# A one-core decoder block: attention steps in a new order, and the memory's query projection moved ahead as a projection of raw x

## The chip, the cores and the metric

One core of a Trainium2 chip runs the whole kernel. The metric is the device time of one execution in microseconds (us). Its engines are TensorE (PE, matmuls; PEld is its weight load), VectorE (DVE), ScalarE (ACT), GpSimd (POOL) and SyncE (SP), which here only issues DMAs. Each engine works through its own instructions in the order in which the program holds them.

## The reference, cut to what matters

256 tokens, model width 1024, everything in fp32.

```
h = rmsnorm(x, norm_w);  proj = h @ w_in          # q,k,v of mixers A and B, q of the memory, gates, merge logits
o_a = dilated_mixture(three groups of q,k,v)      # mixer A: 8 heads, softmax over 3 dilations together
o_b = moba_attention(q, k, v)                     # mixer B: 8 heads, here one causal block of 256
kv  = rmsnorm(mem, mem_norm_w) @ w_mem_kv
o_m = softmax(q_m k_m^T / 8) v_m                  # memory: 4 heads, 256 memory tokens
p_i = (o_i * silu(gate_i)) @ w_branch_i           # i = a, b, m
x   = x + (sum_i sigmoid(logit_i + b_i) * p_i) @ w_out
out = rmsnorm(x, final_norm_w)
```

## The kernel before

**Weights come in chunks.** The list `PLAN` holds all weight matrices cut into chunks of 128 x 2048 fp32 (1 MB). The main loop takes one chunk per turn `i`. Each chunk is loaded by SyncE (`load`, three buffers `wraw`), then split into two halves of higher and lower bits: ScalarE casts `wh` (L93, three buffers) and VectorE subtracts to get `wl` (L94, two buffers). TensorE then does 48 matmuls of 128x256 for a projection chunk, for each of two output halves n: 16 with `wh` against the high and low part of the activations (L232, L233), then 8 with `wl` (L235). For values (`tok`: Bv, Av, Mv) the three kinds alternate (L252 to L254).

**Raw x first.** A row's norm is one factor per token, so chunks 0 to 5 (q, k, v of mixer B) multiply the raw x (`xh`, `xl`: x times the norm weight) and the factor is put on afterwards by `evac_b`, with `rb["x"]`, the factor spread over all partitions by a matmul (`spread`, L181). The factor comes from `stats` (L167 ff.): ScalarE squares the two halves of `xn` (x loaded once more by token) and sums each row (L171), VectorE and GpSimd make it the power -1/2, VectorE makes a diagonal matrix `dg`. All chunks from 6 on multiply h itself, `hh` and `hl`, in which tokens are reordered into classes (`CLASSES`); VectorE makes them from x and `rb["x"]` (`make_h` L195, `split_h` L199) while TensorE is in chunks 3 to 6.

**Order.** Up to turn 7 a scheduler may move TensorE's instructions; from turn 8 on (`manual_schedule`) TensorE's order is the order of the code. The other engines are ordered by the scheduler throughout. `PLAN` before: Bq (0, 1), Bk (2, 3), Bv (4, 5), gates of b (6, 7), of a (8, 9), of m (10), Mq, the memory's queries (11), Mk (12), Mv (13), then the nine chunks of mixer A for heads 0 to 3 (14 to 22), nine for heads 4 to 7, then merge logits (L), branch outputs (W) and the output (O).

**Attention steps.** Heads go in pairs. A pair has steps: scores (score matmuls into two PSUM banks, tag `s`, two buffers; then softmax on VectorE and ScalarE, result `u`), trans (transposes of `u` on TensorE, 3 or 4 a head, `pt`; ScalarE copies them to `ptsb`) and pv (probabilities times values into one bank `o`, then `gated`). `chain` gives every step a due slot, two slots per chunk, and `pump` runs the due steps, nearly all in the middle of a chunk, between its two halves. With two slots from step to step, scores, trans and pv of a pair stand in three chunks in a row. Where several fall in one slot, the key `-j` puts the later step of the earlier pair first: pv, trans, scores. Mixer A has four steps: scores of the first 128 queries, then their trans and the scores of the others, then trans of these, then pv. Its scores have two kinds of matmul: those of group 0 in split fp32r (`score`, L296, L297), and those of the dilated groups in plain fp32 on 64x64 pieces (L368).

`split_q` and `split_k` make the split operands of `score`: ScalarE casts, VectorE subtracts. For mixer B they run at turns 7 (heads 0 to 3), 10 and 11 (heads 4 to 7) behind the gates' tanh; for the memory's queries directly out of the PSUM of chunk 11 (`Mq11x`).

## Time and profile before

| | |
|---|---|
| time, median of 3 runs (lowest to highest) | 348.95 us (347.75 to 350.6) |
| the profiled execution's own time | 347.43 us |
| its span in the trace | 345.6 us |
| mean granted TensorE clock | 0.994 |
| busy: TensorE, VectorE, ScalarE | 334.7, 233.0, 208.8 us |
| first matmul of a weight chunk, end of the last `y` matmul | 4.41 us, about 337.8 us |

The span runs from the first to the last instruction; 1.83 us of the time lie around it. TensorE is busy for 97% of the span, so idle time and slow spots on TensorE are what can be taken away without fewer matmuls; an idle VectorE or ScalarE by itself costs nothing.

### The profile page before, as it was taken

The numbers are of one execution on the slowest core, as the hardware profiler recorded it, in microseconds if no ns is written. First come the engines' busy times: TensorE is split into PE (matmuls) and PEld (weight loads), VectorE is DVE, ScalarE is ACT, GpSimd is POOL, SyncE is SP. The second block draws the span as 40 slices with busy tenths as digits, with TensorE's granted clock in tenths as the row PEclk, the third lists the DMA queues.
The fourth block names the chain that finished last, engine by engine and source line by source line (L and its number), as shares of the span: only waits on it lengthen the run. The fifth ranks groups of instructions, "written<-read, shape, count | busy, mean of one in ns | idle before, by whom it ended". The sixth has DMA issues, their size and how long they took to land.

```text
span 345.6 us, 7107 instructions
## 1 busy us (share of the span) xinstructions
PE 334.7 (97%) x2924; PEld 321.1 (93%) x2924; DVE 233.0 (67%) x402; ACT 208.8 (60%) x372; POOL 28.8 (8%) x40
## 2 busy tenths in 40 slices
PE   7999999998999999999999999999999999999992
PEld 4989999998999998999999999999999999999882
DVE  3849969999876576576664557676462856658553
ACT  6767858987765657575566357564633564645322
POOL 2502000000211000000101000010000403000022
PEclk9999999999999999999999999999999999999997
DMA  6998694944335434443453355444135467655003
GB/s 205 330 409 326 248 370 158 391 177 166 138 160 177 155 127 161 155 168 132 169 190 112 133 154 214 139 189 162 61 123 184 143 229 247 235 167 199 0 3 122
DMA packets 12945, 63.33 MB, mean 183 GB/s; under 512 B 1392, under 2 KB 2800, under 8 KB 6640
## 3 DMA queue, kind: packets, MB, share of 16 engines
q1 hardware_dynamic: 12912, 62.88, 50.7%
q8 instruction: 23, 0.38, 0.4%
q14 instruction: 10, 0.08, 0.1%
HBM read 61.82 MB, written 1.05 MB: 182 GB/s over the span
## 4 chain that ended last, share of the span: by engine, by line
PE 80%; ACT 6%; DMA 5%; DVE 4%; issue 2%; SPq 1%; POOL 0%; POOLq 0%; DVEq 0%; ACTq 0%
PE pj L232 15%; PE pj L233 14%; PE pj L235 14%; PE pj L252 5%; PE pj L253 4%; PE pj L254 4%; PE pt L320 3%; PE pw L232 3%; PE pw L233 3%; PE pw L235 3%; DMA wraw<-in_wts 3%; DMA xn<-in_x 2%; PE y L491 2%; PE y L492 2%; PE y L493 2%; ACT wh L93 2%
## 5 line engine op out<-in xcount | busy, mean ns | idle before, releaser
L94 DVE TENSOR_TENSOR wl<-wraw,wh 128x1024 fp32r<-128x1024 f32 (+2 forms) x117 | 129.9, 1147 | 54.1 <-issue 36.4
L93 ACT CAST wh<-wraw 128x1024 fp32r<-128x1024 f32 (+2 forms) x117 | 108.1, 968 | 45.9 <-PE pj L233 33.3
L232 PE MATMUL pj<-hh,wh 128*128 128x256 f32 x480 | 114.5, 281 | 0.0
L233 PE MATMUL pj<-hl,wh 128*128 128x256 f32 x480 | 113.3, 278 | 0.5 <-DVE hl L199 0.5
L232 PEld LDWEIGHTS pj<-hh,wh 128*128 128x128 f32 x480 | 90.3, 188 | 1.0 <-issue 0.6
L233 PEld LDWEIGHTS pj<-hl,wh 128*128 128x128 f32 x480 | 90.4, 188 | 0.7 <-DVE hl L199 0.7
L235 PE MATMUL pj<-hh,wl 128*128 128x256 f32 x480 | 64.8, 278 | 0.0
L235 PEld LDWEIGHTS pj<-hh,wl 128*128 128x128 f32 x480 | 59.4, 188 | 0.0
L252 PE MATMUL pj<-wh,hh 128*128 128x256 f32 x96 | 26.9, 281 | 0.0
L253 PE MATMUL pj<-wl,hh 128*128 128x256 f32 x96 | 26.6, 277 | 0.0
L254 PE MATMUL pj<-wh,hl 128*128 128x256 f32 x96 | 26.6, 277 | 0.0
L321 ACT COPY ptsb<-pt 128x384 f32<-128x384 f32 (+1 forms) x28 | 13.2, 497 | 20.7 <-PE pt L320 20.7
L312 ACT ACTIVATE u<-u,st 128x384 f32<-128x384 f32 (+2 forms) x32 | 16.8, 527 | 10.8 <-DVE st L306 10.8
L252 PEld LDWEIGHTS pj<-wh,hh 128*128 128x128 f32 x96 | 18.0, 188 | 0.1
L253 PEld LDWEIGHTS pj<-wl,hh 128*128 128x128 f32 x96 | 18.0, 188 | 0.0
L254 PEld LDWEIGHTS pj<-wh,hl 128*128 128x128 f32 x96 | 18.0, 188 | 0.0
L314 DVE TENSOR_SCALAR u<-u,st 128x256 f32<-128x256 f32 (+2 forms) x40 | 15.5, 396 | 0.9
L354 POOL TENSOR_SCALAR nba<-con 128x512 f32<-128x512 f32 x8 | 5.0, 624 | 125.1 <-DVE st L306 124.8
L492 PE MATMUL y<-wl,mgh 128*128 128x512 f32 (+1 forms) x40 | 13.9, 348 | 0.0
L491 PE MATMUL y<-wh,mgh 128*128 128x512 f32 (+1 forms) x40 | 13.9, 347 | 0.0
L320 PE MATMUL pt<-con,u 128*128 128x128 f32 x88 | 12.7, 278 | 1.2 <-DVE u L314 1.2
L493 PE MATMUL y<-wh,mgl 128*128 128x512 f32 (+1 forms) x40 | 13.9, 346 | 0.0
(195 smaller groups left out, 549.2 us busy)
## 6 DMA issues: line engine op xcount, KB each, us to landing
wraw<-in_wts SPq DMA_DIRECT2D x48, 1024.0 KB, 4.8
wraw<-in_wts SPq DMA_DIRECT2D x15, 256.0 KB, 5.8
xn<-in_x SPq DMA_DIRECT2D x1, 1024.0 KB, 8.6
memT<-in_memT SPq DMA_DIRECT2D x1, 1024.0 KB, 5.5
memn<-in_mem SPq DMA_DIRECT2D x1, 1024.0 KB, 7.7
xres<-in_xr SPq DMA_DIRECT2D x1, 1024.0 KB, 7.6
wraw<-in_wts SPq DMA_DIRECT2D x2, 512.0 KB, 3.3
out<-ysb SPq DMA_DIRECT2D x4, 256.0 KB, 2.1
```

The costliest lines, as they stand in the source:

```text
L93: nc.scalar.copy(whs[i][:, sl], raws[i][:, sl])
L94: lower[i] = nc.vector.tensor_tensor(wls[i][:, sl], raws[i][:, sl], whs[i][:, sl].bitcast(F32), op=ALU.subtract)
L232: nc.tensor.matmul(ps[:, lo:lo + S], wh[:, k, fs], ah[k], start=(k == 0), stop=False)
L233: nc.tensor.matmul(ps[:, lo:lo + S], wh[:, k, fs], al[k], start=False, stop=False)
L235: nc.tensor.matmul(ps[:, lo:lo + S], wl[:, k, fs], ah[k], start=False, stop=(k == kn - 1))
L252: nc.tensor.matmul(ps[:, lo:lo + S], ah[k], wh[:, k, :], start=(k == 0), stop=False)
L253: nc.tensor.matmul(ps[:, lo:lo + S], ah[k], wl[:, k, :], start=False, stop=False)
L254: nc.tensor.matmul(ps[:, lo:lo + S], al[k], wh[:, k, :], start=False, stop=(k == KD - 1))
L320: nc.tensor.transpose(ps[:, P * j:P * (j + 1)], u[:, P * c:P * (c + 1)], ident)
L491: nc.tensor.matmul(y[t, n][:, 0:w], ht, wh[:, k, cs], start=(kc == 0 and k == 0), stop=False)
L492: nc.tensor.matmul(y[t, n][:, 0:w], ht, wl[:, k, cs], start=False, stop=False)
L493: nc.tensor.matmul(y[t, n][:, 0:w], lt, wh[:, k, cs], start=False, stop=(kc == 3 and k == 1))
```

## The change

Four things change together.

1. **Memory queries from raw x.** `Mq` moves from place 11 to place 6 of `PLAN` and multiplies `xh`, `xl` like chunks 0 to 5. Gates of b, a, m move back by one, to 7 to 11. `evac_b` puts the norm on (two VectorE operations, in class order); `split_q` of it follows at turn 13 out of SBUF. Mixer B's `split_q`, `split_k` are now made at turns 8 (heads 0 to 3) and 11 (heads 4 to 7).
2. **Statistics of x on VectorE.** `xn` comes in two DMAs, one a half, and its squares are summed by VectorE (`tensor_tensor_reduce`) and no longer by ScalarE.
3. **Mixer B's scores two chunks ahead of its transposes** (slots 0, 4, 6 from a chunk earlier on), and in a shared slot the key is now (j + 1) modulo the number of steps: pv, scores, trans.
4. **Mixer A**: the second step has the fp32 matmuls of the dilated groups first (`far`), then the transposes, then the split ones (`near`). The last pair's second transposes are cut into two runs of three, half a chunk apart.

```diff
+    out.append(("Mq", 0, "in", 7168))
     for hf in range(2):
         out.append(("G", ("b", hf), "in", 6656 + 256 * hf))
...
-    out.append(("Mq", 0, "in", 7168))
...
-    nc.sync.dma_start(xn, x_d.rearrange("(t p) d -> p t d", p=P))
+    for t in range(2):
+        nc.sync.dma_start(xn[:, t, :], x_d[P * t:P * (t + 1), :])
...
+            if name == "x":
+
+                nc.vector.tensor_tensor_reduce(nat[:, t, :], nat[:, t, :], nat[:, t, :], scale=1.0, scalar=0.0,
+                                               op0=ALU.mult, op1=ALU.add, accum_out=ssq[:, t:t + 1])
+            else:
+                nc.scalar.activation(nat[:, t, :], nat[:, t, :], AF.Square, accum_out=ssq[:, t:t + 1])
...
-        def scores(par):
+        def banks(par):
             if par == 0:
                 for s in range(2):
                     nbs[s] = tp.tile([P, 512], F32, tag="nb", name="nba")
                     nc.gpsimd.tensor_scalar(nbs[s], tab_a, SLOPES_A[2 * pair + s], 1.0, op0=ALU.mult, op1=ALU.mult)
-            banks = [pa.tile([P, 512], F32, tag="s", name="sa") for _ in range(2)]
+            return [pa.tile([P, 512], F32, tag="s", name="sa") for _ in range(2)]
+
+        def near(ps, par):
+
             for s in range(2):
                 if par == 0:
-                    out = banks[s].rearrange("p (a b) -> p a b", a=2)[:, :, 0:P]
+                    out = ps[s].rearrange("p (a b) -> p a b", a=2)[:, :, 0:P]
                 else:
-                    out = banks[s][:, 0:S]
+                    out = ps[s][:, 0:S]
                 score(out, qkv["Aq", hf, 0], qkv["Ak", hf, 0], s, f, slice(P * par, P * (par + 1)), slice(0, S))
+
+        def far(ps, par):
+
             for g in range(1, 3):
                 for s in range(2):
                     rows = slice(HD * s, HD * (s + 1))
                     for r in range(2):
                         ts = slice(P * par + 64 * r, P * par + 64 * (r + 1))
                         lo = P * (par + 1) + 64 * (g - 1)
-                        nc.tensor.matmul(banks[s][64 * r:64 * (r + 1), lo:lo + 64], view("q", g)[rows, f, ts],
+                        nc.tensor.matmul(ps[s][64 * r:64 * (r + 1), lo:lo + 64], view("q", g)[rows, f, ts],
                                          view("k", g)[rows, f, ts], start=True, stop=True)
+
+        def weigh(ps, par):
             for s in range(2):
                 us[s, par] = tp.tile([P, 512], F32, tag="u", name="u", bufs=4)
-                softmax(banks[s], nbs[s][:, P * (1 - par):P * (4 - par)], us[s, par], 0, 384)
-
-        def trans(par):
-            for s in range(2):
+                softmax(ps[s], nbs[s][:, P * (1 - par):P * (4 - par)], us[s, par], 0, 384)
+
+        def first():
+            ps = banks(0)
+            near(ps, 0)
+            far(ps, 0)
+            weigh(ps, 0)
+
+        def second():
+
+            ps = banks(1)
+            far(ps, 1)
+            trans(0)
+            near(ps, 1)
+            weigh(ps, 1)
+
+        def trans(par, heads=(0, 1)):
+            for s in heads:
...
-        return [lambda: scores(0), lambda: (trans(0), scores(1)), lambda: trans(1), pv]
+        if pair == 3:
+            return [first, second, lambda: trans(1, (0,)), lambda: trans(1, (1,)), pv]
+        return [first, second, lambda: trans(1), pv]
...
-    def chain(pairs, first, each):
+    def chain(pairs, first, each, at=(0, 2, 4, 6)):
...
-                steps.append((first + each * n + 2 * j, -j, fn))
+                slot = (0, 2, 4, 5, 6)[j] if len(fns) == 5 else at[j]
+                steps.append((first + each * n + slot, (j + 1) % len(fns), fn))
...
+        if kind == "Mq":
+
+            for n in range(2):
+                cs = slice(S * n, S * (n + 1))
+                nc.vector.tensor_tensor(t[:, cs].rearrange("p (e r i) -> p e r i", e=2, r=2),
+                                        ps[:, cs].rearrange(CLASSES, e=2, r=2),
+                                        rb["x"].rearrange(CLASSES, e=2, r=2), op=ALU.mult)
+            return
...
-        if i in (7, 10):
-            hf = (i - 7) // 3
+        if i in (8, 11):
+            hf = (i - 8) // 3
...
+        if i == 13:
+            with behind_gate(11):
+                qkv["Mq", 0] = split_q(qkv["Mq", 0], -SCALE, "Mq")
-        nat = kind[0] == "B"
+        nat = i < 7
...
-            chain([pair_steps_b(p) for p in range(4)], 2 * i + 14, 2)
+            chain([pair_steps_b(p) for p in range(4)], 2 * i + 12, 2, (0, 4, 6))
```

What this does to the order on the engines, at three places. First, ScalarE at about 15 to 30 us, before: the split of chunk 2 (four pieces), the two squares of `xn`, the split of chunk 3, the copy of the spread factor, the split of chunk 4.

```order
L93 CAST wh_186<-wraw_99 128x512 x4
L171 ACTIVATE xn,ssq_x<-xn 128x1024 x2
L93 CAST wh_251<-wraw_108 128x512 x4
L183 COPY rb_x<-spread_x 128x256
L93 CAST wh_311<-wraw_248 128x1024 x2
```

The same place with the change:

```order
L93 CAST wh_187<-wraw_99 128x512 x4
L93 CAST wh_252<-wraw_109 128x512 x4
L189 COPY rb_x<-spread_x 128x256
L93 CAST wh_312<-wraw_249 128x1024 x2
L93 CAST wh_369<-wraw_310 128x1024 x2
```

The squares are gone from ScalarE, so the casts of chunk 3 follow those of chunk 2 directly. On VectorE they now stand here, behind the `wl` of chunk 2 and ahead of the diagonal matrix (`ISA` is the reduction and the read of its sum):

```order
L94 TENSOR_TENSOR wl_188<-wraw_99,wh_187 128x512 x4
L174 ISA xn,ssq_x<-xn 128x1024
L174 ISA ssq_x 128x1
L174 ISA xn,ssq_x<-xn 128x1024
L174 ISA ssq_x 128x1
L144 TENSOR_SCALAR ssq_x<-ssq_x 128x2
L94 TENSOR_TENSOR wl_253<-wraw_109,wh_252 128x512
L181 TENSOR_SCALAR dg_x<-con,ssq_x 128x128 x2
```

Before, the place of the four `ISA` rows was empty and VectorE waited there for ScalarE.

Second, TensorE in the middle of chunk 13 (Mv), before: the transposes of mixer B's first pair, then the scores of its second pair.

```order
L254 MATMUL pj_1122<-wh_932,ml 128x256
L320 MATMUL pt<-con,u 128x128 x6
L296 MATMUL sb<-Bk0y_646,Bq0x_640 128x256
L297 MATMUL sb<-Bk0z_652,Bq0x_640 128x256
L296 MATMUL sb<-Bk0y_649,Bq0x_643 128x256
L297 MATMUL sb<-Bk0z_655,Bq0x_643 128x256
```

With the change:

```order
L260 MATMUL pj_1162<-wh_926,ml 128x256
L302 MATMUL sb<-Bk1y_936,Bq1x_930 128x256
L303 MATMUL sb<-Bk1z_942,Bq1x_930 128x256
L302 MATMUL sb<-Bk1y_939,Bq1x_933 128x256
L303 MATMUL sb<-Bk1z_945,Bq1x_933 128x256
L302 MATMUL sb<-Bk1y_936,Bq1x_930 128x128
L303 MATMUL sb<-Bk1z_942,Bq1x_930 128x128
L302 MATMUL sb<-Bk1y_939,Bq1x_933 128x128
L303 MATMUL sb<-Bk1z_945,Bq1x_933 128x128
L326 MATMUL pt<-con,u 128x128 x6
```

The scores that stand here are now those of the third pair (`Bk1`, `Bq1`: heads 4 to 7), ahead of the first pair's transposes; those of the first pair have moved to the middle of chunk 11, those of the second to the middle of chunk 12.

VectorE at about the same time, before: the scaling of the first pair's probabilities (`u`, one row pair for each head), and between the heads the `wl` of chunk 14 and Mk.

```order
L313 RECIPROCAL st<-st 128x1 x2
L314 TENSOR_SCALAR u<-u,st 128x256
L314 TENSOR_SCALAR u<-u,st 128x128
L313 RECIPROCAL st<-st 128x1
L94 TENSOR_TENSOR wl_1012<-wraw_930,wh_1011 128x1024 x2
L633 TENSOR_TENSOR Mk<-pj_1015,rb_m 128x512
L313 RECIPROCAL st<-st 128x1
L314 TENSOR_SCALAR u<-u,st 128x256
L314 TENSOR_SCALAR u<-u,st 128x128
```

With the change, from the gate of chunk 11 on:

```order
L696 SCALAR_TENSOR_TENSOR g_1041<-thg,pj_948 128x512
L312 ISA u,st<-sb,nbb 128x256
L312 ISA st 128x1
L312 ISA u,st<-sb,nbb 128x128
L312 ISA st 128x1
L320 TENSOR_SCALAR u<-u,st 128x256
L320 TENSOR_SCALAR u<-u,st 128x128
L94 TENSOR_TENSOR wl_1046<-wraw_924,wh_1045 128x1024 x2
L671 TENSOR_TENSOR Mk<-pj_1049,rb_m 128x512
```

The `wl` of chunk 14 and Mk have moved behind the first pair's last scaling; ahead of it stand a gate and the reductions (`ISA`) of the second pair.

Third, TensorE at the second step of a mixer A pair (`Ak21y`, `Aq20x` are the split operands of group 0, `Ak`, `Aq` the plain ones of the dilated groups), before:

```order
L235 MATMUL pj_2122<-hh,wl_1971 128x256 x8
L320 MATMUL pt<-con,u 128x128 x6
L296 MATMUL sa<-Ak21y_1956,Aq20x_1883 128x256
L297 MATMUL sa<-Ak21z_1962,Aq20x_1883 128x256
L296 MATMUL sa<-Ak21y_1959,Aq20x_1886 128x256
L297 MATMUL sa<-Ak21z_1965,Aq20x_1886 128x256
L368 MATMUL sa<-Ak_1455,Aq_1339 64x64 x4
L368 MATMUL sa<-Ak_1695,Aq_1604 64x64 x4
L232 MATMUL pj_2122<-hh,wh_1970 128x256
```

With the change:

```order
L241 MATMUL pj_2126<-hh,wl_1975 128x256 x8
L380 MATMUL sa<-Ak_1459,Aq_1379 64x64 x4
L380 MATMUL sa<-Ak_1699,Aq_1608 64x64 x4
L326 MATMUL pt<-con,u 128x128 x6
L302 MATMUL sa<-Ak21y_1960,Aq20x_1887 128x256
L303 MATMUL sa<-Ak21z_1966,Aq20x_1887 128x256
L302 MATMUL sa<-Ak21y_1963,Aq20x_1890 128x256
L303 MATMUL sa<-Ak21z_1969,Aq20x_1890 128x256
L238 MATMUL pj_2126<-hh,wh_1974 128x256
```

The plain fp32 matmuls (64x64 pieces and transposes) now stand next to each other, and the split ones next to the chunk's own.

## Rows read from the trace of the kernel before

**Rows 1.** The page: busy time of TensorE in the span, and the granted clock in 40 slices of the span, in tenths.

```profile
PE 334.7 (97%) x2924; PEld 321.1 (93%) x2924; DVE 233.0 (67%) x402; ACT 208.8 (60%) x372; POOL 28.8 (8%) x40
PEclk9999999999999999999999999999999999999997
```

**Rows 2.** The view of waits for TensorE, the whole span: who waited for whom, us in total, times, longest.

```profile
PE pt L320 <- DVE u L314: 1.2, 2, 1.0
...
PE pj L232 <- ACT wh L93: 0.8, 1, 0.8
...
PE pj L233 <- DVE hl L199: 0.5, 1, 0.5
```

**Rows 3.** TensorE in order of time, chunk 3 and the start of chunks 4 and 5: start, duration, operation, tile, [idle before it, and who ended that].

```profile
23.60 0.39 PE L232 MATMUL pj<-xh,wh 128*128 128x256 f32 x1 [0.80 <-ACT wh L93]
...
25.23 0.59 PE L181 MATMUL spread_x<-dg_x,ones 128*128 128x256 f32 x2
...
25.78 0.28 PE L233 MATMUL pj<-xl,wh 128*128 128x256 f32 x1
...
29.75 0.28 PE L252 MATMUL pj<-wh,xh 128*128 128x256 f32 x1
...
35.19 0.28 PE L252 MATMUL pj<-wh,xh 128*128 128x256 f32 x1
```

**Rows 4.** ScalarE in order of time, 20 to 32 us.

```profile
20.85 1.06 ACT L171 ACTIVATE xn<-xn 128x1024 f32<-128x1024 f32 x1 [2.56 <-DMA xn<-in_x]
...
22.95 2.17 ACT L93 CAST wh<-wraw 128x512 fp32r<-128x512 f32 x4
...
26.52 2.00 ACT L93 CAST wh<-wraw 128x1024 fp32r<-128x1024 f32 x2 [0.29 <-DVE wl L94]
29.93 2.01 ACT L93 CAST wh<-wraw 128x1024 fp32r<-128x1024 f32 x2 [1.41 <-DMA wraw<-in_wts]
```

**Rows 5.** VectorE in order of time, 23 to 44 us.

```profile
23.07 0.17 DVE L143 TENSOR_SCALAR ssq_x<-ssq_x 128x2 f32<-128x2 f32 x1 [4.06 <-ACT xn L171]
...
24.19 0.48 DVE L175 TENSOR_SCALAR dg_x<-con,ssq_x 128x128 f32<-128x128 f32 x2
...
27.61 2.69 DVE L94 TENSOR_TENSOR wl<-wraw,wh 128x1024 fp32r<-128x1024 f32 x2 [0.54 <-ACT wh L93]
...
40.95 1.25 DVE L94 TENSOR_TENSOR wl<-wraw,wh 128x1024 fp32r<-128x1024 f32 x1
42.09 1.25 DVE L199 TENSOR_TENSOR hl<-h,hh 128x1024 fp32r<-128x1024 f32 x1
```

**Rows 6.** TensorE in order of time, in chunks 6 and 7, where it first needs the second half of `hl`.

```profile
43.39 0.38 PE L233 MATMUL pj<-hl,wh 128*128 128x256 f32 x1 [0.47 <-DVE hl L199]
```

**Rows 7.** TensorE in order of time, the middle of chunk 13: the six transposes of mixer B's first pair, then the first score matmul of its second pair.

```profile
83.67 0.49 PE L320 MATMUL pt<-con,u 128*128 128x128 f32 x3
85.19 0.55 PE L320 MATMUL pt<-con,u 128*128 128x128 f32 x3 [1.03 <-DVE u L314]
85.50 0.36 PE L296 MATMUL sb<-Bk0y,Bq0x 128*128 128x256 f32 x1
```

**Rows 8.** VectorE in order of time, 61 to 90 us: the memory's statistics, one of two splits of Mq, the `wl` of chunk 14, Mk, the last scaling of mixer B's first pair, two of the four softmax reductions of its second pair.

```profile
61.68 0.17 DVE L143 TENSOR_SCALAR ssq_m<-ssq_m 128x2 f32<-128x2 f32 x1 [0.34 <-ACT memn L171]
...
78.15 0.69 DVE L272 SCALAR_TENSOR_TENSOR Mq11x<-pj,Mq11x 64x512 fp32r<-64x512 f32 x1
...
81.56 2.34 DVE L94 TENSOR_TENSOR wl<-wraw,wh 128x1024 fp32r<-128x1024 f32 x2
83.93 0.69 DVE L633 TENSOR_TENSOR Mk<-pj,rb_m 128x512 f32<-128x512 f32 x1
...
84.61 0.53 DVE L314 TENSOR_SCALAR u<-u,st 128x256 f32<-128x256 f32 x2
...
88.92 0.42 DVE L306 CUSTOM_DVE_ANT_0 u<-sb,nbb 128x256 f32<-128x256 f32 x1
...
89.27 0.28 DVE L306 CUSTOM_DVE_ANT_0 u<-sb,nbb 128x128 f32<-128x128 f32 x1
```

**Rows 9.** TensorE in order of time, the eight transposes of the memory's second pair, in the middle of chunk 20.

```profile
137.07 0.77 PE L320 MATMUL pt<-con,u 128*128 128x128 f32 x5
138.03 0.55 PE L320 MATMUL pt<-con,u 128*128 128x128 f32 x3 [0.20 <-DVE u L314]
138.33 0.36 PE L232 MATMUL pj<-hh,wh 128*128 128x256 f32 x1
```

**Rows 10.** TensorE in order of time, the second step of a mixer A pair, from the end of its six transposes to the chunk's next matmuls.

```profile
163.58 0.36 PE L296 MATMUL sa<-Ak21y,Aq20x 128*128 128x256 f32 x1
163.79 0.28 PE L297 MATMUL sa<-Ak21z,Aq20x 128*128 128x256 f32 x1
...
164.03 0.28 PE L297 MATMUL sa<-Ak21z,Aq20x 128*128 128x256 f32 x1
164.24 0.46 PE L368 MATMUL sa<-Ak,Aq 64*64 64x64 f32 x16
164.63 0.38 PE L232 MATMUL pj<-hh,wh 128*128 128x256 f32 x1
164.85 0.29 PE L233 MATMUL pj<-hl,wh 128*128 128x256 f32 x1
```

**Rows 11.** Groups of VectorE instructions by line and shape, the whole span: busy us, mean ns of one | idle before.

```profile
L306 DVE CUSTOM_DVE_ANT_0 u<-sa,nba 128x384 f32<-128x384 f32 x16 | 8.3, 555 | 7.9 <-PE sa L368 7.9
```

More of the change, by code (lines that the diff above doesn't have):

```diff
@@ L170, in stats @@
         for t in range(2):
-            nc.scalar.activation(nat[:, t, :], nat[:, t, :], AF.Square, accum_out=ssq[:, t:t + 1])
+            if name == "x":
[3 more added lines that the diff above has]
+                nc.scalar.activation(nat[:, t, :], nat[:, t, :], AF.Square, accum_out=ssq[:, t:t + 1])
         r = rstd_of(ssq, name)
@@ L571 @@
                 split(i + 2, j, 4 if i < 2 else 2)
-        if i in (7, 10):
-            hf = (i - 7) // 3
+        if i in (8, 11):
+            hf = (i - 8) // 3
             with behind_gate(i - 1):
                 qkv["Bqx", hf] = split_q(qkv["Bq", hf], 1.0, f"Bq{hf}")
-                if i == 7:
-                    qkv["Bkx", hf] = split_k(qkv["Bk", hf], f"Bk{hf}")
-        if i == 11:
-            with behind_gate(9):
-                qkv["Bkx", 1] = split_k(qkv["Bk", 1], "Bk1")
+                qkv["Bkx", hf] = split_k(qkv["Bk", hf], f"Bk{hf}")
         if i in (9, 10):
@@ L614 @@
                         split(i + 2, 1, 2)
-        if kind[0] == "B":
+        if i < 7:
             late.append((i, kind, key) + ((pss[2 * i], pss[2 * i + 1]) if i < 2 else (ps, None)))
@@ L620 @@
                     late.remove(z)
-                if i > 3:
+                if i in (4, 5):
                     split_h(4 * i - 16, 4 * i - 12)
```

## The prediction, made before the change was run

> **What bounds the kernel now.** I read the page first: TensorE is busy for 97% of the span at full granted clock until the last slice [rows 1], so the time is TensorE's own work plus the few places where it stands. The waits of TensorE alone [rows 2] name three engines' work it waited for: transposes for VectorE's scaled probabilities, a projection for ScalarE's weight cast, another for VectorE's `hl`. These three sum to 2.5 us; beside them it waits only in its first 6 us, which the change leaves alone. So no order of steps can bring more than this and what TensorE loses around the waits. I then read each place in order of time on TensorE and on the engine it waits for [rows 3 to 9], and last the places where TensorE never waits and still is slower than its pitch [rows 10]. The pitch: chunk 4 has 48 matmuls and runs from 29.75 to 35.19 [rows 3], 5.44 us, or 0.113 us a matmul. The number of matmuls does not change, so the gain is the sum of the stalls that go, less those that come.
>
> **A. Start of chunk 3.** TensorE was ready at 22.80 and began at 23.60 behind ScalarE's cast; chunk 4 began at 29.75 [rows 3], 6.95 us later than 22.80. Needed are 48 x 0.113 = 5.44 and the spread matmul, 25.78 - 25.23 less one pitch = 0.44: 5.88 together. So 1.07 us are lost: 0.80 of waiting, and 0.27 in which casts of 2.17 / 4 = 0.54 each pace matmuls that want a piece every 0.46. ScalarE was late because it squared `xn` from 20.85 to 22.95, after waiting 2.56 us for xn's DMA [rows 4]. Without the squares it can cast as soon as chunk 3 lands. That landing has no row; all four pieces were there when the casts ran from 22.95 on without a pause, and a cast begun by 22.26 is in time.
> The new risk is the spread matmul, which now stands behind 8 of chunk 3's matmuls, so TensorE comes to it at 22.80 + 0.91 = 23.71. It needs the diagonal matrix, which was ready at 24.19 + 0.48 = 24.67, 1.6 us after the sums at 23.07 [rows 5]. No row shows a VectorE reduction of 1024 elements. Nearest are the softmax reductions, 0.28 us at 128 columns, 0.42 at 256 [rows 8], 0.555 at 384 [rows 11]: 0.14 for each further 128 gives 1.26. VectorE is free from 23.07 - 4.06 = 19.01. If the first half of xn has landed by 19.6 (my estimate: one half of the DMA earlier than the whole, which landed at 20.85) and the second lands with the whole, the sums end at 20.85 + 1.26 + 0.1 = 22.2 and the diagonal at 23.8: a wait of 0.1. If both halves land only at 20.85, the sums end at 23.5, the diagonal at 25.1, a wait of 1.4. I take the first.
> Then chunk 4 sets the limit. ScalarE's first cast of it began at 26.52 after a wait put down to VectorE's `wl`, but that `wl` is chunk 3's, which this cast doesn't need; so it was chunk 4's own DMA, which doesn't move. VectorE's first half of `wl` follows at 27.61 + 1.25 = 28.86 [rows 5], TensorE wants it with its second matmul: chunk 4 begins at 28.75 at the earliest. **Gain 1.0** of 1.07; bounds 1.07 and -0.35.
>
> **B. `hl` in chunk 6.** TensorE waited 0.47 us and its next matmul was 0.10 slower [rows 6]: 0.57. The memory's queries now fill this place with raw x and need no `hl`. VectorE's order from 27.61 to 43.34 is unchanged and starts from the same DMA, so `hl` ends at 42.09 + 1.25 = 43.34 as before [rows 5], while chunk 7, which wants it, begins at 28.75 + 3 x 5.44 = 45.1: covered by 1.7 us. Chunk 6 itself wants the second half of its `wl`, ready at 40.95 + 1.25 = 42.2, at its 23rd matmul, 39.63 + 2.5 = 42.1: a wait of 0.1 at most. The two new VectorE operations that put the norm on replace, later, the reading of PSUM in two splits of 0.69 [rows 8]; VectorE has time for them. **Gain 0.6**, bounds 0 and 0.6. TensorE is then 1.6 us ahead.
>
> **C. First transposes of mixer B.** Three transposes took from 83.67 to 85.19, the next three 0.31 [rows 7]: 1.2 us lost. Whether it comes back is VectorE's affair, which hardly pauses from 61.68 to the end of that scaling at 84.61 + 0.53 = 85.14 [rows 8]. In the new order this stretch loses two splits of Mq (2 x 0.69), the `wl` of chunk 14 (2.34) and Mk (0.69), 4.4 us; it gains the second pair's reductions (2 x 0.70) and one gate (as Mk, 0.69), 2.1 us. It ends at 85.14 - 2.3 = 82.8 if it begins at 61.68 again, which hangs on ScalarE's squares of `mem` and its queue of casts. TensorE comes to the middle of chunk 13 at 83.67 - 1.6 + 0.9 (one more group of 8 score matmuls stands ahead) = 83.0; first the third pair's scores, which need the second pair's reductions out of the way of the PSUM banks (82.8 - 0.53 = 82.3, cover 0.7), then at 83.9 the transposes (cover 1.1). Behind the scores no one waits but TensorE itself and all its projections. **Gain 1.2**, less 0.2 for a cover this thin; bounds 1.2 and the loss of the slow rival below.
>
> **D. Transposes of the memory's second pair.** Eight took 138.33 - 137.07 = 1.26; at 0.10 each, as the last three [rows 9], they take 0.8. The scores of that pair now go ahead of the first pair's transposes, so its softmax starts some 0.8 us earlier, more than the wait. **Gain 0.4**, bounds 0 and 0.46.
>
> **E. Fewer changes between plain fp32 and split matmuls.** In a second step of mixer A, the matmul behind the transposes takes 163.79 - 163.58 = 0.21 instead of 0.12, the first plain one 164.24 - 164.03 = 0.21, and back 164.85 - 164.63 = 0.22 [rows 10]: three changes of 0.09 to 0.10. With `far` and the transposes side by side two are left. Counting stretches of plain work on TensorE in both orders, mixer A has 18 before and 13 now (with one more for the cut transposes), mixer B 5 and 6. Four stretches fewer at 0.09 to 0.19 are 0.4 to 0.75 us. **Gain 0.4**; bounds 0 (if the cost hangs on the shape alone) and 0.75.
> [...]
>
> **Sum.** 1.0 + 0.6 + 1.2 - 0.2 + 0.4 + 0.4 = 3.4 us. Against the profiled execution: 347.43 - 3.4 = 344.0. That execution lies 1.5 us under the median of 348.95, and the change has nothing to alter that scatter, so the median comes to **345.6**. Nothing after the memory's pairs but E changes, and the 1.83 us outside the span stay.
>
> **Rivals.**
> *Squares slow on VectorE.* If a reduction with both inputs in SBUF runs at half speed, 2.5 us each, the second ends at 24.7, the diagonal comes at 26.3 and TensorE waits 2.6 us: 345.6 + 2.6 = 348.2. For it: no row has such an operation. Against: subtractions with both inputs in SBUF take 1.25 at 1024 [rows 5], as the extrapolation. [...] Chance 0.13.
> *The stall moves.* TensorE, 1.6 us earlier, meets a VectorE and DMAs that are no earlier from 27 to 45 us: any of the covers of 0.1 in A and B that fails hands the gain back. Then A and B bring 0.2: 345.6 + 1.4 = 347.0. For it: VectorE runs there without a pause. Chance 0.13.
> *VectorE late in chunk 13, slower than before.* If ScalarE's casts keep the second pair's reductions at their old time, 89.27 + 0.28 = 89.55 [rows 8], the third pair's scores find no bank and TensorE stands from 83.0 on for 6.5 us: 345.6 + 6.5 = 352.1. It is slower than before from a wait of 3.4 us on. Against: 2.3 us of work have been taken out from ahead of them. Chance 0.04.
>
> **How the numbers follow.** The forecast has 0.70, its own range 344.4 to 346.8 (E at its bounds, C without its 0.2, half a us of scatter). For 8 in 10 the range goes from 343.9 (all gains at their upper bounds, scatter) to 348.1, which takes in the two rivals that lose the start. One per cent, about what a measurement of this kernel tells from none, is 3.5 us, under 345.46: the forecast lies on that edge, a little above. So faster by over 1% gets 0.43 of it, slower by over 1% (above 352.4) 0.03, within 0.54.
>
> **What would show it.** On TensorE no wait before chunk 3, in chunk 6 and in the middles of chunks 13 and 20; chunk 4 beginning near 28.75; the spread matmul without a wait of over 0.2; the sums of x ended by 22.3; two slow changes a second step. Wrong would be a reduction of 1024 columns near 2.5 us, a wait of TensorE at scores of mixer B, or a new one for `wl` between 28 and 50 us.

## The result, and the profile after

The changed kernel takes 345.75 us (median of 6 runs, 344.76 to 347.16), the kernel before beside it 348.75: a ratio of 0.992 (0.990 to 0.995). A second comparison gave 345.52 against 348.20, 0.992 (0.988 to 0.995). So it is 2.7 to 3.0 us faster, 0.8%, and the forecast of 345.6 came true to 0.15 us. How it came true is another matter: the forecast's own sum ran from the profiled execution, 347.43, to 344.0, and the changed kernel's profiled execution took 346.01. One of the five terms brought nothing, the saving of another was taken back, and what decides most was not among them. The intervals leave out two executions, of 1178 and 676 us, that stand far above all others of their kernels.

The page of the changed kernel, the rows that answer to [rows 1]:

```profile
PE 335.4 (97%) x2924; PEld 322.2 (94%) x2924; DVE 235.9 (69%) x408; ACT 206.3 (60%) x368; POOL 28.8 (8%) x40
...
PEclk9999999999999999999999999999999999999997
```

And the view of waits for TensorE, to set beside [rows 2] (us in total, times, longest):

```profile
PE pwarm L138 <- DVE zero L108: 1.0, 1, 1.0
PE pj L251 <- ACT wh L93: 0.6, 1, 0.6
PE spread_x L187 <- DVE dg_x L181: 0.2, 1, 0.2
```

All three waits of [rows 2] are gone: `u`, `hl` and ScalarE's cast ahead of chunk 3. New is 0.2 us at the spread matmul (0.1 was forecast); the 0.6 us is for weights of the first chunk that landed late, and ends at 10.6 us. Yet TensorE's busy time, which holds no waits, *rose* from 334.7 to 335.4 us, at a mean granted clock of 0.994 in both spans. That row points at what decides the case.

To see where the time went I cut the trace of each kernel at the same four places on TensorE: the start of chunk 4, the end of the memory's last pv, the end of mixer A's last pv (each taken as the start of the matmul behind it), and the first output matmul.

| us | first projection to chunk 4 | to the memory's end | to mixer A's end | to the output |
|---|---|---|---|---|
| before | 25.34 | 115.43 | 109.01 | 62.68 |
| changed | 25.35 | 114.14 | 108.20 | 62.68 |
| changed, second profile | 24.99 | 114.14 | 108.20 | 62.68 |

The first stretch swings from run to run; the others come out the same to 0.01 us in the two profiles of the changed kernel, and so they tell tenths apart that no median can. The gain is 1.29 between chunk 4 and the memory, 0.81 in mixer A, and nothing at the start or the end: 2.10, and TensorE's last matmul starts 1.98 earlier on the clock of the two profiles (338.91 and 336.93; its end in the kernel before, which the table ahead of the prediction puts at about 337.8, lies at 339.2). The end of VectorE's last scaling moved by 2.27, since VectorE's last wait for ScalarE shrank from 0.81 to 0.52, but the span by 1.4 only: what follows that scaling, the last output transfer, took 0.85 us longer. This is no scatter. The view of DMA queues from the issue of the last two output transfers to the end (queue: packets, MB, share of 16 engines), before and then changed:

```profile
q1 hardware_dynamic: 288, 0.52, 39.7%
```

```profile
q1 hardware_dynamic: 288, 0.52, 31.7%
q14 instruction: 1, 0.01, 1.2%
```

In the changed kernel a load of 8 KB of instructions falls into the output transfer. It does so in seven of the 13 profiles of this document, and there the last transfer lands 2.8 to 3.0 us after its issue; in the other six that load starts 0.9 us or more ahead of these issues, and the transfer lands after 2.05 to 2.06. The seven are both profiles of the changed kernel and those of its variants that keep the squares on VectorE and the queries on raw x; the six are the kernel before, its variants, and the three kernels below that have the squares or the queries put back. No run moves the load by itself, so that it is the cause is argued and not shown; but a span set against one of those three is off by some 0.9 us in their favour. The medians say 2.7 to 3.0; what is over 2.3 of that has no place in the traces.

**The start of chunk 3.** The changed kernel's ScalarE, then VectorE, then TensorE in order of time, to set beside [rows 3 to 5]:

```profile
22.22 2.53 ACT L93 CAST wh<-wraw 128x512 fp32r<-128x512 f32 x4 [2.95 <-DMA wraw<-in_wts]
...
26.68 2.00 ACT L93 CAST wh<-wraw 128x1024 fp32r<-128x1024 f32 x2 [0.80 <-DMA wraw<-in_wts]
```

```profile
19.93 1.23 DVE L174 CUSTOM_DVE_ANT_0 xn<-xn 128x1024 f32<-128x1024 f32 x1
...
21.28 1.23 DVE L174 CUSTOM_DVE_ANT_0 xn<-xn 128x1024 f32<-128x1024 f32 x1
...
24.18 0.48 DVE L181 TENSOR_SCALAR dg_x<-con,ssq_x 128x128 f32<-128x128 f32 x2 [0.61 <-POOL ssq_x L145]
```

```profile
23.51 0.28 PE L238 MATMUL pj<-xh,wh 128*128 128x256 f32 x1
...
24.81 0.67 PE L187 MATMUL spread_x<-dg_x,ones 128*128 128x256 f32 x2 [0.22 <-DVE dg_x L181]
...
29.87 0.28 PE L258 MATMUL pj<-wh,xh 128*128 128x256 f32 x1
```

The reductions of 1024 columns take 1.23 us (the extrapolation gave 1.26) and end at 22.51. ScalarE casts chunk 3 as soon as it lands, at 22.22. But TensorE comes to chunk 3 only at 23.51, 0.7 later than the 22.80 of before, held up by weights in its first 20 us. ScalarE's casts of chunk 2, before (the first piece of this row is still chunk 1's) and then changed, end at 15.04 + 3.25 = 18.29 and 16.67 + 2.61 = 19.28:

```profile
15.04 3.25 ACT L93 CAST wh<-wraw 128x512 fp32r<-128x512 f32 x5 [1.38 <-DMA wraw<-in_wts]
```

```profile
16.67 2.61 ACT L93 CAST wh<-wraw 128x512 fp32r<-128x512 f32 x4 [0.63 <-DMA wraw<-in_wts]
```

And the diagonal matrix is ready at 24.18 + 0.48 = 24.66, no earlier than before (24.67 [rows 5]): VectorE waited 0.61 us for GpSimd's power, which took 1.27 us instead of 0.72 (GpSimd's spans are rough). From start to start the spread matmul held TensorE up 0.46 us more than before. So chunk 4 begins at 29.87 against 29.75 [rows 3].

**Mixer B and the memory.** TensorE at the places of [rows 7] and [rows 9]:

```profile
85.95 0.84 PE L326 MATMUL pt<-con,u 128*128 128x128 f32 x6
...
136.52 1.09 PE L326 MATMUL pt<-con,u 128*128 128x128 f32 x8
137.36 0.37 PE L238 MATMUL pj<-hh,wh 128*128 128x256 f32 x1
```

The six transposes go in one run, and the eight take 137.36 - 136.52 = 0.84 instead of 1.26.

**What was not in the sum.** In both kernels the matmuls of a projection follow each other at one of two intervals, and keep to it for a whole block. The row that holds the last eight matmuls of a block is 1.07 us long at the one and 1.11 at the other; from start to start it is 113.3 ns (10.88 us for 96) and 117.8 (11.31 for 96). TensorE in chunks 6 to 8, before and then changed:

```profile
47.01 1.07 PE L235 MATMUL pj<-hh,wl 128*128 128x256 f32 x8
48.71 1.07 PE L235 MATMUL pj<-hh,wl 128*128 128x256 f32 x8
51.43 1.07 PE L235 MATMUL pj<-hh,wl 128*128 128x256 f32 x8
```

```profile
45.70 1.11 PE L241 MATMUL pj<-xh,wl 128*128 128x256 f32 x8
...
51.12 1.11 PE L241 MATMUL pj<-hh,wl 128*128 128x256 f32 x8
53.95 1.11 PE L241 MATMUL pj<-hh,wl 128*128 128x256 f32 x8
```

The changed kernel runs chunks 6 to 10 and half of 11, 264 matmuls, at the longer interval: 264 x 4.5 ns = 1.2 us, of which the kernel before pays less than 0.1, for the 18 matmuls of chunk 6 ahead of its wait for `hl`. It eats more than that wait had cost (0.57).

### The profile page after: what moved, and what is told of

Its sections match the earlier page's. It is cut to its first block, busy times and chain, and to the rows that moved or that the text cites. A ratio compares the mean times of both kernels' runs of the same rounds, so it can differ in the third digit from the quotient of the medians.

```text
span 344.2 us, 7110 instructions
## 1 busy us (share of the span) xinstructions
PE 335.4 (97%) x2924; PEld 322.2 (94%) x2924; DVE 235.9 (69%) x408; ACT 206.3 (60%) x368; POOL 28.8 (8%) x40
## 4 chain that ended last, share of the span: by engine, by line
PE 90%; DMA 5%; DVE 1%; SPq 1%; POOL 1%; issue 0%; POOLq 0%; DVEq 0%
PE pj L238 17%; PE pj L241 17%; PE pj L239 17%; PE pj L258 5%; PE pj L260 5%; PE pj L259 5%; PE pt L326 3%; DMA wraw<-in_wts 3%; PE pw L238 3%; PE pw L239 3%; PE pw L241 3%; DMA xn<-in_x 2%; PE y L522 2%; PE y L523 2%; PE y L524 2%; PE oa L415 1%
## 5 line engine op out<-in xcount | busy, mean ns | idle before, releaser
L238 PE MATMUL pj<-hh,wh 128*128 128x256 f32 x464 | 110.8, 280 | 0.0
L239 PE MATMUL pj<-hl,wh 128*128 128x256 f32 x464 | 109.6, 278 | 0.0
L238 PEld LDWEIGHTS pj<-hh,wh 128*128 128x128 f32 x464 | 87.4, 188 | 0.7 <-issue 0.6
L239 PEld LDWEIGHTS pj<-hl,wh 128*128 128x128 f32 x464 | 87.4, 188 | 0.0
L241 PE MATMUL pj<-hh,wl 128*128 128x256 f32 x464 | 62.8, 278 | 0.0
L241 PEld LDWEIGHTS pj<-hh,wl 128*128 128x128 f32 x464 | 57.6, 188 | 0.0
L312 DVE CUSTOM_DVE_ANT_0 u<-sa,nba 128x384 f32<-128x384 f32 x16 | 8.3, 555 | 7.1 <-PE sa L303 3.8
```

The source lines that it names most:

```text
L238: nc.tensor.matmul(ps[:, lo:lo + S], wh[:, k, fs], ah[k], start=(k == 0), stop=False)
L239: nc.tensor.matmul(ps[:, lo:lo + S], wh[:, k, fs], al[k], start=False, stop=False)
L241: nc.tensor.matmul(ps[:, lo:lo + S], wl[:, k, fs], ah[k], start=False, stop=(k == kn - 1))
```

## The experiments

### One part undone at a time

Four kernels, each the changed one with one part put back.

```diff
 # squares of x back on ScalarE
-            if name == "x":
-                nc.vector.tensor_tensor_reduce(nat[:, t, :], nat[:, t, :], nat[:, t, :], ...)
-            else:
-                nc.scalar.activation(nat[:, t, :], nat[:, t, :], AF.Square, accum_out=ssq[:, t:t + 1])
+            nc.scalar.activation(nat[:, t, :], nat[:, t, :], AF.Square, accum_out=ssq[:, t:t + 1])
```

> The changed kernel with the squares of x back on ScalarE (x still comes in two halves). By my step A (the squares held up ScalarE's casts of chunk 3) TensorE waits some 0.8 us for a cast ahead of chunk 3 again, chunk 4 begins about 1.0 us later than 29.87, and the time rises from 345.75 to about 346.7. By the rival (the landing of the weights of chunks 3 and 4 paces TensorE there, whoever squares) the wait before chunk 3 may return, but chunk 4 begins within 0.2 us of 29.87 and the time stays within 0.3 us.

Measured: 344.83 us, 0.991 (0.988 to 0.993); no slower than the changed kernel. The wait is back, and chunk 4 does begin 1.5 us later than in the changed kernel. TensorE:

```profile
24.92 0.39 PE L233 MATMUL pj<-xh,wh 128*128 128x256 f32 x1 [0.85 <-ACT wh L93]
...
31.35 0.28 PE L253 MATMUL pj<-wh,xh 128*128 128x256 f32 x1
```

Half a us of that came before chunk 3, and the next stretch is shorter: 113.40 against 114.14, because here chunks 4 and 5 ran at 117.8 ns and chunks 6 to 10 at 113.3. TensorE's way from the first projection to the last output matmul is 1.2 us longer (333.64 against 332.42). So neither theory was right: the wait costs, but the profile's time does not show it, for the interval gave back 0.74, and the last output transfer, without the load of instructions, 0.9.

```diff
 # the memory's queries back behind the gates (and Bq, Bk splits at chunks 7, 10, 11)
-    out.append(("Mq", 0, "in", 7168))
     for hf in range(2):
         out.append(("G", ("b", hf), "in", 6656 + 256 * hf))
...
     out.append(("G", ("m", 0), "in", 7424))
+    out.append(("Mq", 0, "in", 7168))
...
```

> The changed kernel with the memory's queries back in their old place behind the gates, made from the normalized hh and hl, and the splits of mixer B's queries and keys back at their old chunks. By my step B the first matmul on hl stands in chunk 6 again, waits 0.4 to 0.5 us for VectorE and is 0.1 slower: the time rises by 0.6 to about 346.3, and nothing else waits, since VectorE's two splits (2 x 0.69) fit into the 1.7 us that it has in hand at mixer B's third scores. By the rival (the cover there is used up) a wait on VectorE of 0.3 to 1.5 us comes on top near 85 us: 346.6 to 347.8. By a third reading (what is gained at hl is lost again in the next chunks) the wait returns and the time does not change.

Measured: 345.34 us, 0.992 (0.989 to 0.994). The wait for `hl` is there, 0.45 us, and no wait for VectorE came with it; by the medians the time did not change. The trace says more: the stretch from chunk 4 to the memory's end takes 115.21 us instead of 114.14. Ahead of the wait chunk 6 ran at 113.3 ns (15 matmuls in 1.70 us), behind it at the long interval, as did chunks 7 to 10:

```profile
43.79 0.39 PE L239 MATMUL pj<-hl,wh 128*128 128x256 f32 x1 [0.45 <-DVE hl L205]
44.72 1.10 PE L241 MATMUL pj<-hh,wl 128*128 128x256 f32 x8
```

So undoing B cost 1.07 us here. The profile's span hides it (344.3 us against 344.2): this kernel's last output transfer, too, is without the load of instructions.

```diff
 # mixer B's old slots and order
-            chain([pair_steps_b(p) for p in range(4)], 2 * i + 12, 2, (0, 4, 6))
+            chain([pair_steps_b(p) for p in range(4)], 2 * i + 14, 2, old=True)
...
```

> The changed kernel with mixer B's steps in their old slots and order: scores one chunk ahead of their transposes. By my step C the first transposes of the mixer wait about 1.0 us for VectorE's scaling again: 345.75 + 1.2 = 346.9 or so. By the rival (it is the memory's queries, taken out of VectorE's stretch from 61 to 85 us, that made u early: 85.14 less two splits of 0.69 is 83.8, when TensorE comes at 83.7 to 84.0) they wait 0.3 us at most, and the time stays within 0.4 us.

Measured: 347.79 us, 0.9995 (0.997 to 1.002): 2.0 us lost, more than expected. TensorE waits twice for `u`:

```profile
84.82 1.01 PE L326 MATMUL pt<-con,u 128*128 128x128 f32 x6 [1.11 <-DVE u L320]
...
93.91 0.30 PE L326 MATMUL pt<-con,u 128*128 128x128 f32 x1 [0.71 <-DVE u L320]
```

The second wait is one that the kernel before doesn't have. VectorE shows why: between the second pair's reductions and its last scaling now stand the splits of the memory's queries, which the change has put at chunk 13, and the `wl` of a chunk:

```profile
89.19 1.49 DVE L278 SCALAR_TENSOR_TENSOR Mqx<-Mq,Mqx 64x512 fp32r<-64x512 f32 x2
...
90.85 2.34 DVE L94 TENSOR_TENSOR wl<-wraw,wh 128x1024 fp32r<-128x1024 f32 x2
...
93.24 0.99 DVE L320 TENSOR_SCALAR u<-u,st 128x256 f32<-128x256 f32 x4
```

So the place of the queries' splits suits the new slots and not the old ones; the rival, that the slots don't matter, is out.

```diff
 # mixer A's second step as before, no cut of the fourth pair's transposes, the old order in a shared slot
+            trans(0)
             ps = banks(1)
+            near(ps, 1)
             far(ps, 1)
-            trans(0)
-            near(ps, 1)
...
-        if pair == 3:
-            return [first, second, lambda: trans(1, (0,)), lambda: trans(1, (1,)), pv]
...
-            chain([pair_steps_a(2 * key[0] + p) for p in range(2)], 2 * i + 2, 4)
+            chain([pair_steps_a(2 * key[0] + p) for p in range(2)], 2 * i + 2, 4, old=True)
```

> The changed kernel with mixer A's steps as before: transposes, near, far in the second step, the old order of steps that fall on one slot, and the last transposes of the fourth pair in one step. By my step E five stretches of plain fp32 work come back at 0.09 to 0.19 each: 0.4 to 0.7 us, 346.2 to 346.5. [...] From the second steps' own times in the two traces (1.62 before, 1.58 after) I would rather expect 0.03 to 0.1 a step, 0.1 to 0.3 in all.

Measured: 346.21 us, 0.9945 (0.992 to 0.997), 0.46 us above the changed kernel's 345.75, with an interval that overlaps that one's. The stretch to mixer A's end tells it apart: 109.21 us against 108.20, 1.0 us, of which 0.4 is that 374 instead of 285 matmuls have the long interval, and 0.6 the changes. E's lower bound of 0, for a cost that hangs on the shape alone, is out; so is my 0.1 to 0.3. In the changed kernel's second step, the matmul behind the transposes (same 128x128 shape, another type) still holds up its successor by 163.36 - 163.16 = 0.20, 0.09 more than the pitch:

```profile
162.53 0.87 PE L326 MATMUL pt<-con,u 128*128 128x128 f32 x6
163.16 0.37 PE L302 MATMUL sa<-Ak21y,Aq20x 128*128 128x256 f32 x1
163.36 0.28 PE L303 MATMUL sa<-Ak21z,Aq20x 128*128 128x256 f32 x1
```

### Two parts undone at once, one part done alone

The changed kernel with the first two edits above together:

> The changed kernel with two parts undone at once: the squares of x on ScalarE and the memory's queries in their old place. By my steps A and B this costs 1.0 + 0.6 = 1.6 us, a ratio of about 0.9965 to the kernel before, and the two waits (0.8 for ScalarE's cast ahead of chunk 3, 0.5 for hl in chunk 6) are back. By the reading that each of the two undone alone suggests (ratios of 0.9909 and 0.9917 against 0.9923 for the whole) they cost nothing: 0.992, though the waits are back. A third reading: one hides the other, so that only the later wait costs: 0.6, about 0.9935.

Measured: 345.85 us, 0.993 (0.990 to 0.996), beside 345.52 for the changed kernel in the same comparison. The wait for `hl` has grown, since this time the start was quick (24.63 us to chunk 4), and behind it the matmuls are at the short interval:

```profile
43.41 0.38 PE L234 MATMUL pj<-hl,wh 128*128 128x256 f32 x1 [1.09 <-DVE hl L200]
...
47.05 1.07 PE L236 MATMUL pj<-hh,wl 128*128 128x256 f32 x8
48.75 1.07 PE L236 MATMUL pj<-hh,wl 128*128 128x256 f32 x8
```

The stretch from chunk 4 takes 114.41 us with a wait of 1.09, and 114.14 without any. The wait and the slow matmuls beside it cost 1.4 us, of which 1.1 came back: 257 matmuls at the long interval instead of 502. For the wait turned the interval here from long to short; with the queries alone put back it turned it from short to long, and a shorter wait cost 1.07.

> The changed kernel as it is, on the chip of the next three, so that all four have one measure. 345.75 give or take 0.5, 0.992 of the kernel before. In its profile the matmuls of chunks 4 to 10 should again follow at one of two intervals, 113.3 or 117.8 ns, and which of them rules from about 16 to 72 us need not be the one of the first profile (117.8 from chunk 6 on): if it is chance, another profile can differ there by up to 1.5 us.

The changed kernel again gave 345.52 and the same interval in the same chunks. But it hangs on the start. Two kernels of this document, the one with mixer A's old steps and the one below with the split matmuls last, have the same order on TensorE until 154 us; both began chunk 4 at the long interval, and their stretches to the memory's end took 114.55 and 113.40 us instead of 114.14.

```diff
 # the kernel before, with mixer B's new slots alone
-            chain([pair_steps_b(p) for p in range(4)], 2 * i + 14, 2)
+            chain([pair_steps_b(p) for p in range(4)], 2 * i + 12, 2, (0, 4, 6), True)
```

> The kernel before with one part of the change alone: mixer B's scores two chunks ahead of its transposes, in the order pv, scores, transposes. By my step C, as sized, 1.2 us less than before: 0.9965. By what its undoing cost (2.0 us, two waits on u of 1.11 and 0.71), 2 us less: 0.994. By the rival of VectorE late in chunk 13 (here the memory's queries are still in VectorE's way) the third pair's scores wait for a bank: a wait of TensorE at scores of over 0.5 us, and 0.998 or more.

Measured: 346.66 us, 0.996 (0.994 to 0.998), 1.5 us less than before. The stretch from chunk 4 is 114.09 instead of 115.43: 1.34, of which 0.3 is a shorter wait for `hl` (0.2 instead of 0.47, after a late start). No scores waited; the transposes still waited 0.2. This is step C by itself, at 1.0, or 1.2 with the interval taken out (284 matmuls at the long one instead of 258).

### The interval

Tabulating in the traces which interval ruled ahead of each step and which behind, I had a guess that steps which end in plain fp32 make the next block slow. So I put the split matmuls last (`far`, then `near` in the first step, with the third step's transposes ahead of it, and the cut dropped):

```diff
-            near(ps, 0)
             far(ps, 0)
+            near(ps, 0)
...
-        if pair == 3:
-            return [first, second, lambda: trans(1, (0,)), lambda: trans(1, (1,)), pv]
...
-            chain([pair_steps_a(2 * key[0] + p) for p in range(2)], 2 * i + 2, 4)
+            chain([pair_steps_a(2 * key[0] + p) for p in range(2)], 2 * i + 2, 4, rank=(2, 2, 1, 0))
```

> The changed kernel with mixer A's first step turned round (far ahead of near), the third step's transposes ahead of it, and the fourth pair's last transposes in one run again: wherever near stands, it is the last of its step. In the traces so far a projection block behind a step that ends in plain fp32 has its matmuls at 117.5 to 122 ns, one behind near at 113.3 to 113.5. If the last matmul of a step sets that, the blocks behind the four first steps (2 of 48, 2 of 24 and 24 more each) speed up by 4 to 8 ns a matmul and two stretches go: about 1.0 to 1.4 us less than the changed kernel, 344.5. If the cost is only that of the changes between plain and split (0.1 to 0.2 each), one or two of which go: 0.1 to 0.3 less. [...]

Measured: 347.71 us, 0.999 (0.997 to 1.001): 2.2 us *slower* than the changed kernel. No expectation held. Mixer A's stretch was as in the changed kernel (108.29), but the last one took 65.11 us instead of 62.68. Every projection from 251 us on had the long interval. The table of transitions, read again, is of another kind: a run of six plain transposes by itself *turns* the interval, whichever it was (18 times of 18 over the 13 profiles of this document); a run of three leaves it (16 of 16); between two blocks with no step between them it stays (in all 473 places from chunk 4 on), except where a chunk with the activations as weights is followed by one with the weights as weights, where it mostly turns (91 of 106). That gave two predictions with opposite signs.

```diff
 # the changed kernel, the fourth pair's last six transposes in one run
-        if pair == 3:
-            return [first, second, lambda: trans(1, (0,)), lambda: trans(1, (1,)), pv]
```

> The changed kernel with one edit: the fourth pair's last six transposes in one step again, not in two runs of three. By the count of stretches in my step E a plain stretch less should save 0.1 to 0.2 us: 345.4. By the reading of the eight traces so far (a run of six transposes turns the interval of the matmuls behind it from 113.3 to 117.8 ns or back, a run of three leaves it, and nothing turns it again from some 252 us to the end of the projections at 315) all 528 matmuls there now run at 117.8 ns: 2.4 us more, about 347.9, and the stretch from mixer A's last pv to the output chunks takes 65.1 instead of 62.7 us.

Measured: 348.74 us, 1.000 (0.998 to 1.003): the whole gain gone. The last stretch takes 65.11 us. TensorE around the cut and at the start of two later blocks, 96 matmuls apart, in the changed kernel and then with one run of six:

```profile
243.60 1.07 PE L241 MATMUL pj<-hh,wl 128*128 128x256 f32 x8
244.51 0.49 PE L326 MATMUL pt<-con,u 128*128 128x128 f32 x3
...
246.67 1.07 PE L241 MATMUL pj<-hh,wl 128*128 128x256 f32 x8
247.58 0.49 PE L326 MATMUL pt<-con,u 128*128 128x128 f32 x3
...
255.05 0.28 PE L238 MATMUL pj<-hh,wh 128*128 128x256 f32 x1
...
265.93 0.28 PE L238 MATMUL pw<-ogm,wh 128*128 128x256 f32 x1
```

```profile
245.07 1.07 PE L241 MATMUL pj<-hh,wl 128*128 128x256 f32 x8
245.98 0.82 PE L326 MATMUL pt<-con,u 128*128 128x128 f32 x6
...
248.52 1.11 PE L241 MATMUL pj<-hh,wl 128*128 128x256 f32 x8
...
256.79 0.28 PE L238 MATMUL pj<-hh,wh 128*128 128x256 f32 x1
...
268.09 0.28 PE L238 MATMUL pw<-ogm,wh 128*128 128x256 f32 x1
```

The same 96 matmuls take 265.93 - 255.05 = 10.88 and 268.09 - 256.79 = 11.30 us. It is not the granted clock: the view by stretches of that kernel (stretch, its length, TensorE's busy time and instructions, granted clock, DMA share, GB/s) has it at 1.00, as the changed kernel's has:

```profile
256.50:267.50 11.00, 11.00 (x95) 1.00 0.43 146
```

```profile
256.50:267.50 11.00, 11.00 (x99) 1.00 0.41 144
```

The kernel before, with the cut and nothing else:

```diff
+        if pair == 3:
+            return [lambda: scores(0), lambda: (trans(0), scores(1)), lambda: trans(1, (0,)), lambda: trans(1, (1,)), pv]
...
```

> The kernel before with one edit: the fourth pair's last six transposes cut into two runs of three, as the change has them. There the projection ahead of them runs at 117.8 ns and the one behind at 113.3. By the same reading the cut takes away the turn, the matmuls to the end stay at 117.8 ns, and the kernel is 2.4 us slower than before, a ratio of 1.007. By the count of stretches one is added: 0.1 to 0.2 us, 1.0005. If the cut makes TensorE fast by itself: no change, since it is fast there already.

Measured: 351.15 us, 1.007 (1.004 to 1.010), as the turning says. The block ahead of these transposes is slow in the kernel before; one run of six turns it to fast for all that follows, and the cut takes that away (65.12 us for the last stretch). So by the last stretch the same edit is worth 2.4 us in one order and costs 2.4 in the other. Last, the place where the interval turned in chunk 6:

```diff
+            if n == "v" and hf:
+                out.append(("Mq", 0, "in", 7168))
             out.append(("B" + n, hf, "in", b0 + 512 * i + (256 * hf if i else 0)))
-    out.append(("Mq", 0, "in", 7168))
...
```

> The changed kernel with the memory's queries between the two chunks of mixer B's values instead of behind them, so that the step from a chunk with the weights moving to one with the weights standing, which turned the interval in 65 of 80 places, comes twice instead of once ahead of the gates. If chunk 4 begins at 113.3 ns, then chunks 5 and 6 are slow and 7 to 10 fast, instead of 6 to 10 slow: 0.7 to 0.8 us less, 344.8, with the stretch from chunk 4 to the memory's pairs shorter by that. If chunk 4 begins at 117.8 ns, it is chunks 5 and 6 that are fast and 7 to 10 slow: 0.6 us more than the changed kernel would take from that start. If the interval has nothing to do with such steps: the same time, 345.6.

Measured: 345.20 us, 0.990 (0.987 to 0.993), not to be told from the changed kernel by medians. The stretch from chunk 4 is 113.44 instead of 114.14, 0.70 less, as expected, and TensorE shows the two halves of chunk 5 slow and those of chunk 7 fast:

```profile
37.64 1.10 PE L242 MATMUL pj<-xh,wl 128*128 128x256 f32 x8
40.47 1.11 PE L242 MATMUL pj<-xh,wl 128*128 128x256 f32 x8
...
48.94 1.07 PE L242 MATMUL pj<-hh,wl 128*128 128x256 f32 x8
51.66 1.07 PE L242 MATMUL pj<-hh,wl 128*128 128x256 f32 x8
```

With the interval known, the lengths of the stretches can be freed of it. In each trace I counted the matmuls of projections whose successor starts some 117.8 ns later, and took 4.5 ns off for each:

| us | chunk 4 to the memory's end | long ones | freed | to mixer A's end | long ones | freed |
|---|---|---|---|---|---|---|
| before | 115.43 | 258 | 114.27 | 109.01 | 329 | 107.53 |
| changed | 114.14 | 502 | 111.88 | 108.20 | 285 | 106.92 |
| squares back | 113.40 | 336 | 111.88 | 108.20 | 284 | 106.92 |
| memory's queries back | 115.21 | 580 | 112.60 | 108.20 | 285 | 106.92 |
| both back | 114.41 | 257 | 113.26 | 108.20 | 283 | 106.92 |
| mixer B's old slots | 116.32 | 481 | 114.16 | 108.20 | 285 | 106.92 |
| before, mixer B's new slots alone | 114.09 | 284 | 112.81 | 109.00 | 328 | 107.52 |
| mixer A's old steps | 114.55 | 598 | 111.86 | 109.21 | 374 | 107.53 |
| split matmuls last | 113.40 | 337 | 111.88 | 108.29 | 282 | 107.01 |

Freed of the interval, kernels that share a part agree on it to 0.02 us. The change takes 114.27 - 111.88 = 2.39 us of waits and slow matmuls out of the first stretch and 0.61 out of the second; the interval gives 1.1 of the first back and adds 0.2 to the second.

## Why the prediction was right, and where it was not

The number held because errors cancelled. Of the 3.4 us of the sum, A brought nothing; B, C and D together brought 2.39 instead of 2.0, and E 0.6 instead of 0.4. Against these 3.0 stand 0.9 lost to the interval and 0.85 at the last output transfer, neither of which was in the sum, and the profiled span shrank by 1.4. That the medians moved by 2.7 to 3.0 all the same, and met the forecast, is luck as far as the traces go.

- **A, start of chunk 3** (gain 1.0): the mechanism held, the gain did not show. ScalarE's cast no longer waits for squares, and the reduction's 1.23 us confirm the extrapolation, so the rival of slow squares is out: no run shows the 2.5 us that it took for a reduction at half speed. The step that failed is the one that took TensorE's arrival at chunk 3 (22.80; it came at 23.51) and the diagonal (23.8; it was ready at 24.66) for settled. Over 13 profiles the way from the first projection to chunk 4 took 25.7 us on average with the squares on ScalarE (24.6 to 27.3, five profiles) and 25.5 with them on VectorE (24.7 to 27.2, eight): it swings by more than the term, so that no gain of A can be told from these. The sums came at 22.5, not 22.2, for the second half of `xn` landed at 21.26 and not by 20.85; the wait at the spread matmul was 0.2, and 0.46 from start to start.
- **B, `hl`** (0.6): the wait went, no cover failed; chunk 7 came late enough. Freed of the interval, the wait with its slow matmuls costs 0.72 where it is 0.45 long and 1.38 where it is 1.09, so the term was right. But "the stall goes" is not "the time goes": the wait had turned the interval in chunk 6, in the kernel before to the short one, and without it TensorE stayed at 117.8 ns. Undoing B cost 0.27 us (with the squares put back too) where chunk 4 had begun at the short interval, and 1.07 where it had begun at the long one.
- **C, mixer B** (1.2 less 0.2): 1.0 alone (1.2 freed of the interval), and 2.18 by undoing it (116.32 against 114.14), because the queries' splits, moved to chunk 13, make a second wait in the old order. The term was right for the step by itself; that the parts lean on each other was left out. The covers of 0.7 and 1.1 were wider in the event: VectorE's scaling ended at 83.99, TensorE came to the scores at 85.08. VectorE late in chunk 13 never happened.
- **D, the memory's second pair** (0.4): 1.26 - 0.84 = 0.42, read from the rows; it was not undone by itself, but B's 0.72, C's 1.2 and this make 2.3 of the 2.39.
- **E, fewer changes** (0.4): 0.81 between the two traces, 1.0 by undoing it. Freed of the interval both are 0.61: five stretches fewer in mixer A, 0.12 each, a little over the 0.1 that I took for it. The lower bound of 0, for a cost that hangs on the shape alone, was a supposition that no run shows; the trace disagrees, with 0.09 behind the transposes at an unchanged 128x128 shape.
- **The cut transposes**: counted as one more stretch, at 0.1 to 0.2. They decide the interval of all that follows, 2.4 us. It isn't a gain over the kernel before, which had the short interval there by its own order, but without it the changed kernel would have been no faster. The step that failed here is the first of the prediction: I took a pitch of 0.113 from chunk 4 [rows 3] for a constant, and compared no second block with it.
- **The stall moves** was the rival that came nearest the truth in kind: B's gain was handed back, to TensorE's own interval and not to VectorE or a DMA; A's went to chunk 2's weights, which landed later, and to the diagonal.
- **After the memory's pairs** the prediction had nothing but E change. The last output transfer did, by 0.85.

Open: what in TensorE makes the two intervals, why six transposes turn them and three don't, and what sets the interval at chunk 4. The runs show the rule, not its cause. Open too is a part of the medians' 2.7 to 3.0 us, of which the traces account for 2.0 to 2.3 up to the last scaling, and for 1.4 with the output.

## What to carry to other kernels

When a kernel is at 97% of one engine, look at the engine's own interval before its waits: compare the length of equal blocks through the whole trace, and if they come in two sizes, find what switches between them, for here one switch ahead of the last stretch moved 2.4 us, and a wait for `hl` of 1.09 us with its slow matmuls 1.38. Undo each part by itself, and cut the traces at fixed places: lengths that, freed of the interval, repeat to 0.02 us separate what medians that scatter by 2 us cannot. When undoing a part seems to cost nothing, look at the start and the end of the trace before calling the part worthless: here the end of the kernel had changed with it. A sum that comes out right is no proof of its terms.

## What the hardware showed that I had not expected

- Projection matmuls of 256 columns follow at 113.3 or 117.8 ns, at a granted clock of 1.00 for both, and keep to one for up to 60 us. In 13 profiles a lone run of six transposes turned the interval 18 times of 18; a run of three kept it 16 times of 16; a change of chunk with no step between kept it in all 473 places from chunk 4 on, except from a chunk with activations as weights to one with weights as weights, where it turned in 91 of 106: always from the short to the long interval (28 of 28), and in 63 of 78 the other way.
- A wait of TensorE can turn the interval too, either way. All four profiles with a wait for `hl` in chunk 6 show it: three turned to the short interval there, one to the long. So 1.09 us of waiting cost 0.27 us in one kernel, and 0.45 us of waiting cost 1.07 in another.
- The last output transfer lands 2.05 us after its issue, or 2.8 to 3.0 where an 8 KB load of instructions falls into it (seven of 13 profiles, and none of the other six), which moves a span by some 0.85.
